# Attention loop: projections in half steps of three matmuls, other gaps between the blocks of logits

## The chip, the cores and the metric

One core of a Trainium2 chip runs the whole program. The metric is the device time of one execution in microseconds, from the median of several runs. The kernel is built with a planner (a tile framework): the program says what is computed and in which order of preference, and the planner lays out each engine's queue from its own estimate of times. Each engine then runs its queue in order, and waits at semaphores for the others. TensorE (PE) multiplies, VectorE (DVE) and ScalarE (ACT) work on results in PSUM and SBUF, SyncE (SP) issues DMAs, and GpSimd (POOL) is little used here.

## What is computed

A decoder trunk of two layers on 1024 tokens of width 1024: an RG-LRU layer, then a layer of attention with a forget gate (16 heads of 64), each with a SiLU gate, and a final RMS norm. The change is in the attention layer, of which this is the core:

```python
def one_block(args):
    q_blk, cq_blk, start = args
    qpos = start + jnp.arange(Q_BLOCK, dtype=jnp.int32)
    logits = jnp.einsum("bqhd,bkhd->bhqk", q_blk.astype(jnp.float32), kf) * scale
    logits = logits + (cq_blk[..., :, None] - ck[:, :, None, :])
    mask = kpos[None, :] <= qpos[:, None]
    logits = jnp.where(mask[None, None], logits, NEG_INF)
    p = jax.nn.softmax(logits, axis=-1)
    return jnp.einsum("bhqk,bkhd->bqhd", p, vf)

y = o * jax.nn.silu(gate)
return y @ w_out.astype(h.dtype)
```

`q`, `k`, `v` and `gate` are projections of the normed input, `ck` is a running sum of the log of the forget gate. All is float32 in the reference.

## The kernel before

Every float32 product is made of three matmuls of split operands (high times high, low times high, high times low), so that a product over 128 rows of a weight is a group of three matmuls.

**The attention loop** runs over 16 heads. For each head the 1024 queries are eight blocks of 128, and block i needs keys 0 to (i + 1) x 128. Blocks 0 to 3 are the small half, 4 to 7 the large half. The loop body of head `hd` has two calls of `run`: the first lays the large half of `hd` beside the weighting of its small half, the second lays the small half of `hd + 1` beside the weighting of the large half of `hd`. So on TensorE large and small halves alternate.

**A block of logits** is one step of the generator `maxima`: two matmuls into the PSUM tile `S` for a small block and four for a large one (by chunks of keys), mask and row maximum on VectorE (L965, output `m`), the exponential on ScalarE (`p<-S,m`), the sum's reciprocal on VectorE (L976, L977), the normalised halves `pp` (the high part on ScalarE, the low part on VectorE, L979), and a DMA transpose on SP's queue into `pT` (L982). `S` has two buffers, each of two PSUM banks, and `p` has two as well. So the logits of a block can start when the exponential two blocks earlier is through, and an exponential when the low part two blocks earlier is.

**The weighting** is the generator `weigh`: it multiplies `pT` with the values into the PSUM tile `O`, in two steps (small half) or four (large half). Its first matmul needs the transposes of all four blocks of the half.

**The fill.** Between these, TensorE makes the projections that later heads need: `play` walks over units (the gate, keys or queries of a pair of heads for 512 tokens, tile `gps`), each of 24 matmuls of 512 columns. `gemm_steps` hands control back after every second group of three, so a step is six matmuls, and a unit four steps. At the end of a unit VectorE scales its result (L692), and `use` splits it, for keys and queries into the tiles `kq` (`qkh`, `qkl`). In heads 12 to 15 the fill goes over to the last gate units, the output projection (`partial`) and `turned`.

**The order** is written out by hand, a string for each call of `run`: "1" is a block of logits, "0" a step of the weighting, "." a step of the fill. Heads 0 to 11 use `ORDER`, heads 12 to 15 `LAST`. Each step is pinned behind the last matmul issued (`tc.issue_after(pe[0].ins)`), so that TensorE's queue follows the string; the other engines' queues are the planner's.

**The loads beside it.** `side` is advanced once after each ".": it issues the loads `pieces` that copy the next heads' queries (to `U`, in the first call) and keys (to `T`, in the second) from `kq` on SP's queue, two to four DMAs a step. Each is pinned behind the transpose issued three before the latest (`turns[-lag]`, lag 3). A tile of `kq` is overwritten by a later unit only when the loads that read it are through. In heads 3, 7 and 11 `vals` (the generator `values`) is advanced behind the first and the third block of the second call: it loads and casts the weights of the next four heads' values; their 192 matmuls (`vps`) follow after that call.

**The weights.** `play` loads the next unit's weights when `i == u["load"]`, and casts them when `i` is in `u["cast"]`, where `i` counts the yields of the current unit.

Of the kernel before, what the change touches and what calls it, by code (L numbers as in the profile page):

```python
# [25 lines left out]
HD = 64  # L26
EPS = 1e-6
GROUP = 2
ORDER = "1.1..1.1..00", "1.1.1.1...0000"
LAST = "1..1..1..1..0.0", "1..1.1..1..0..0.0.0"  # L30
NEG = -1e30
PSUM = bass.MemoryType.PSUM
# [8 lines left out]
def trunk(ctx: ExitStack, tc: tile.TileContext, xt, w0, wg, wo0, pc, gn, gf, w1, wv, wf, bf, wo1, out):  # L41
# [95 lines left out]
    def gemm_steps(ps, pairs, chunks=(slice(0, HALF),)):  # L137

        pairs = list(pairs)
        for cs in chunks:  # L140
            o = ps[:, cs]
            for i, ((wh, wl), (xh, xl)) in enumerate(pairs):
                matmul(o, wh, xh[:, cs], start=i == 0, stop=False)
                matmul(o, wl, xh[:, cs], start=False, stop=False)
                matmul(o, wh, xl[:, cs], start=False, stop=i == len(pairs) - 1)
                if i % 2:
                    yield

    def drain(gen):
        for _ in gen:  # L150
# [2 lines left out]
    def take(gen, n):  # L153
        for _ in range(n):
            next(gen, None)
# [464 lines left out]
    with ExitStack() as l1:  # L620
# [49 lines left out]
        plan = []  # L670

        def job(w, h, start, use):
            u = dict(w=w, h=h, start=start, use=use, load=0, cast=(1, 2))
            plan.append(u)
            return u

# [97 lines left out]
        def kq_units(pair, parts):  # L774

            units = []
            for is_k, hs in parts:
                if hs[0] == 0 or pair == 0 or is_k and pair in (3, 5, 7):
                    kqw[is_k] = Weights(is_k * 8 + pair)

                def start(is_k=is_k, first=[True]):
                    if is_k not in kq:
                        kq[is_k] = tuple(
                            kqpool.tile([P, SEQ], F32R, tag=f"qk{p}{is_k}", name=f"qk{p}") for p in "hl"
                        )

                def use(h, pt, is_k=is_k):
                    cs = halves[h]
                    hi, lo = kq[is_k]
                    if is_k:  # L790
                        to_hi(hi[:, cs], pt, nc.scalar)
                        to_lo(lo[:, cs], pt, hi[:, cs], nc.vector)
                    else:
                        to_hi(hi[:, cs], pt, nc.scalar, scale=0.125)
                        nc.vector.scalar_tensor_tensor(lo[:, cs], pt, 0.125, f32(hi[:, cs]), ALU.mult, ALU.subtract)  # L795

                new = [job(kqw[is_k], h, start, use) for h in hs]
                for u in new:
                    u["first"], u["last"] = hs[0], hs[-1]
                    if is_k and hs == (0,) and pair in (3, 5, 7):  # L800
                        u["load"], u["cast"] = 2, (2, 3)
                units += new
            return units

# [232 lines left out]

        def run(order, *gens, fill=iter(()), side=iter(()), vals=None):

            for n, i in enumerate(order):  # L1040
                if vals and n in (1, 5):
                    with tc.issue_after(turns[-1].ins):
                        next(vals)
                if vals and n == order.rfind("1"):
                    next(vals)
                    behind[:] = loaded_last[0], cast_last[0]
                with tc.issue_after(pe[0].ins):
                    next(fill if i == "." else gens[int(i)], None)
                if i == ".":
                    next(side, None)  # L1050
            for g in gens:
                drain(g)

# [23 lines left out]
        def beside(steps, first, more):  # L1077

            for i, _ in enumerate(steps):
                if i >= first:  # L1080
                    next(more, None)
                yield

# [65 lines left out]
        def turned(c, q):  # L1149
# [14 lines left out]
            for b in range(2):  # L1164
# [4 lines left out]
                for h, (d0, nd) in enumerate(parts):  # L1169
# [6 lines left out]
                    for k in range(2):  # L1176
# [4 lines left out]
                        matmul(pt, yh, wl, start=False, stop=k == 1)  # L1181
                        if k == 0:
                            yield
                    sq = at.tile([P, HALF], F32, tag="pp", name="sq1", bufs=4)[:, : nd * P]
                    nc.scalar.activation(sq, pt, AF.Square, accum_out=ss[:, min(h, ss.shape[1] - 1)].unsqueeze(1))
                    if c == 0 or h < len(parts) - 1:
                        nc.vector.tensor_tensor(res[b][:, hs], pt, grow[d0 // 4][:, (d0 % 4) * P : (d0 % 4 + nd) * P], ALU.mult)  # L1187
                        if h == 1 and c == 1:
                            nc.vector.tensor_tensor(ss[:, 0:1], ss[:, 0:1], ss[:, 1:2], ALU.add)
                            ss = ss[:, 0::2]  # L1190
                        yield
                if c == 1:
                    r = root_mean(ss, lambda: nc.vector.tensor_tensor(res[b][:, hs], pt, grow[d0 // 4][:, (d0 % 4) * P : (d0 % 4 + nd) * P], ALU.mult))  # L1193
                    lo, hi = halves
                    nc.scalar.activation(res[b][:, lo], res[b][:, lo], AF.Copy, scale=r)
                    nc.vector.tensor_scalar(res[b][:, hi], res[b][:, hi], r, None, ALU.mult)
                    for hs in halves:
                        nc.sync.dma_start(out[4 + 2 * q + b, :, hs], res[b][:, hs])
                    yield
            if c == 0:  # L1200
                first_half.extend(res)
# [38 lines left out]
        gates1 = forget(1)  # L1240
        for _ in range(2):
            next(gates1)
            take(fill, 2)
        drain(gates1)
        drain(fill)
        fill = play(next(fills))
        for _ in range(4):
            next(fill)
        load(0, halves[1], (1,))
        load(1, halves[1], (1,))  # L1250
# [133 lines left out]
```

## Time and profile before

| | us |
|---|---|
| median of 3 runs | 1064.38 |
| lowest and highest | 1063.75, 1068.48 |
| the profiled execution's span, first to last instruction | 1057.4 |
| attention loop, heads 0 to 15, about | 506 to 1029 |
| of it heads 0 to 11, which use `ORDER`, about | 506 to 894 |

The profiled execution's whole time is its span and what lies before the first and behind the last instruction of the program. The rows of the profile that matter are shown with the prediction. How to read them: a row of the time line has the start, the duration, the engine, the line of the kernel, the operation, out<-in by the program's names, the shape, the count of instructions merged into the row, and in brackets the idle time of the engine before it and what ended that. Busy times of matmuls overlap, since they are pipelined and their ends are modelled. A row of the waits has who waited for whom, the total in us, the number of times and the longest. A row of the stretches has the stretch, its length, the busy time and count of each engine (PE, PEld, DVE, ACT, POOL), TensorE's granted clock, the share of the DMA engines and GB/s. L69 is the helper that all matmuls go through and L57 the one of all activations, so the tiles tell what an instruction is: `S<-T,U` logits, `gps<-h,w` the fill, `O<-pT,v` the weighting, `vps<-w,h` the values, `p<-S,m` an exponential, `pp<-p,sums` a normalised block.

### The profile page before, as it was taken

What the parts mean: (1) busy time and instruction counts of PE and PEld (TensorE: products, weight loads), DVE (VectorE), ACT (ScalarE), POOL (GpSimd) and SP (SyncE); (2) the same over time, 40 slices, a digit from 0 to 9 for tenths busy, and PEclk for the clock granted to TensorE, in tenths of its full rate; (3) what the DMA queues carried; (4) which work ended last, traced back from release to release, by engine and by line L of the source; (5) the groups of instructions that cost most, each with busy time, mean ns of one, the idle gap of its engine ahead of it and who ended that gap; (6) DMA issues with size and microseconds to landing.
All of it is one profiled execution on the core that took longest, in us unless ns stands there. A gap on an engine that the chain in (4) does not pass through costs nothing. (4 is left out here: it accounts for less than half of the span.)

```text
span 1057.4 us, 15071 instructions
## 1 busy us (share of the span) xinstructions
PE 1022.6 (97%) x5094; PEld 710.3 (67%) x5094; DVE 786.5 (74%) x1456; ACT 660.7 (62%) x1211; POOL 90.6 (9%) x87
## 2 busy tenths in 40 slices
PE   9999999999999999998999989999999999999997
PEld 6787878888888888765444456444754448477676
DVE  7789657667856868895879875888578875986575
ACT  8479666565657565567656755666466764854455
POOL 1311112012101120001000000000000000012100
PEclk9999999999999999999999999999999999999999
DMA  7112424233423311443688993898748985789984
GB/s 246 61 50 63 124 84 144 68 115 108 133 66 113 122 50 48 161 141 75 150 166 169 185 208 70 182 192 175 182 95 189 176 190 133 168 196 250 230 199 160
DMA packets 219806, 148.92 MB, mean 141 GB/s; under 512 B 161937, under 2 KB 174865, under 8 KB 219729
## 3 DMA queue, kind: packets, MB, share of 16 engines
q1 hardware_dynamic: 217328, 140.09, 54.0%
q0 software_dynamic: 2400, 7.87, 2.5%
q8 instruction: 40, 0.66, 0.2%
q14 instruction: 38, 0.30, 0.1%
HBM read 73.33 MB, written 11.67 MB: 80 GB/s over the span
## 5 line engine op out<-in xcount | busy, mean ns | idle before, releaser
L69 PE MATMUL gps<-h,w 128*128 128x512 f16 x1152 | 269.1, 380 | 1.3 <-DVE qkl L795 1.1
L69 PEld LDWEIGHTS <-w 128*128 128x128 f16 x1152 | 104.2, 98 | 126.8 <-issue 14.0
L57 ACT ACTIVATE p<-S,m 128x128 f32<-128x128 f32 (+7 forms) x128 | 94.4, 738 | 78.0 <-DVE m L965 32.4
L57 ACT ACTIVATE pp<-p,sums 128x128 f16<-128x128 f32 (+7 forms) x128 | 96.6, 770 | 34.9 <-DVE sums L977 22.0
L979 DVE SCALAR_TENSOR_TENSOR pp<-p,sums,pp 128x128 f16<-128x128 f32 (+7 forms) x128 | 102.5, 812 | 13.5 <-ACT pp L57 12.4
L69 PE MATMUL S<-T,U 96*128 96x512 f32 (+7 forms) x384 | 106.4, 386 | 5.2 <-ACT p L57 4.1
L965 DVE CUSTOM_DVE_ANT_0 S<-S,mask 128x128 f32<-128x128 f32 (+7 forms) x128 | 96.9, 758 | 11.8 <-PE S L69 10.5
L69 PE MATMUL vps<-w,h 128*128 128x256 f16 (+1 forms) x768 | 90.6, 280 | 11.4 <-ACT w L57 7.4
L110 POOL TENSOR_TENSOR wl<-wf,wh 128x512 fp32r<-128x512 f32 x46 | 69.3, 1511 | 324.5 <-ACT wh L57 268.5
L69 PEld LDWEIGHTS <-h 128*128 128x128 f16 x768 | 76.3, 100 | 25.9 <-issue 9.9
L69 PEld LDWEIGHTS S<-T,U 128*128 128x128 f32 (+1 forms) x384 | 66.9, 189 | 39.3 <-ACT p L57 19.1
L57 ACT CAST wh<-wf 128x512 fp32r<-128x512 f32 x88 | 51.6, 592 | 51.1 <-PE ops L69 27.6
L69 PE MATMUL ups<-hh,wh 128*128 128x512 f32 x192 | 76.2, 398 | 1.1 <-ACT hh L57 1.0
L69 PE MATMUL ops<-yh,wh 128*128 128x512 f32 x192 | 76.7, 399 | 0.6 <-ACT yh L57 0.6
L69 PE MATMUL ups<-hh,wl 128*128 128x512 f32 x192 | 75.7, 394 | 1.0 <-POOL wl L110 1.0
L69 PE MATMUL ups<-hl,wh 128*128 128x512 f32 x192 | 76.2, 397 | 0.2
L69 PE MATMUL ops<-yh,wl 128*128 128x512 f32 x192 | 75.7, 394 | 0.1
L69 PE MATMUL gps<-hh,wh 128*128 128x512 f32 x192 | 75.7, 394 | 0.1
L69 PE MATMUL gps<-hh,wl 128*128 128x512 f32 x192 | 75.5, 393 | 0.0
L69 PE MATMUL gps<-hl,wh 128*128 128x512 f32 x192 | 75.5, 393 | 0.0
L403 DVE TENSOR_TENSOR x<-x,ops 128x512 f32<-128x512 f32 x80 | 54.0, 679 | 28.2 <-PE ops L69 27.9
L69 PE MATMUL ops<-yl,wh 128*128 128x512 f32 x192 | 74.6, 394 | 0.0
(196 smaller groups left out, 1877.9 us busy)
## 6 DMA issues: line engine op xcount, KB each, us to landing
wf<-in_w SPq DMA_DIRECT2D x106, 256.0 KB
wsf<-in_w SPq DMA_DIRECT2D x48, 256.0 KB
wf<-in_wo SPq DMA_DIRECT2D x64, 128.0 KB
T<-qkh SPq DMA_DIRECT2D x64, 128.0 KB
U<-qkh SPq DMA_DIRECT2D x64, 128.0 KB
x<-in_xt SPq DMA_DIRECT2D x16, 256.0 KB
wsf<-in_wv SPq DMA_DIRECT2D x16, 256.0 KB
x1d<-x SPq DMA_DIRECT2D x16, 256.0 KB
```

The lines of the kernel that those rows point to most:

```text
L57: act[0] = op(*args, **kw)
L69: pe[0] = nc.tensor.matmul(*args, **kw)
L110: return eng.tensor_tensor(lo, src, f32(hi), ALU.subtract)
L403: nc.vector.tensor_tensor(x, x, pt, ALU.add)
L965: nc.vector.tensor_tensor_reduce(S[:, :n], S[:, :n], mask[:, SEQ - n :], -1.0, -NEG, ALU.add, ALU.min, accum_out=m)
L979: nc.vector.scalar_tensor_tensor(both[:, :, 1], p, r, both[:, :, 0], ALU.mult, ALU.subtract)
```

## The change

`gemm_steps` hands control back after every group of three matmuls, a half step. In the order strings "." stays a step (two half steps), and "," is new, one half step. `ORDER` becomes, between blocks, a step and a half, a step, a step and a half and two steps, in both calls; before it was 1, 2, 1, 2 steps in the first call and 1, 1, 1, 3 in the second. The sum is six steps in each, as before. `LAST` is unchanged. Whatever counted steps counts half steps: `load` and `cast` of the units, `beside`, the doubled yields in `turned`, the counts in front of the loop. `side` is advanced each time that the count of half steps since the start of the call is even after a "." or ",". `vals` is advanced behind the first and the third block by counting blocks.

```diff
-ORDER = "1.1..1.1..00", "1.1.1.1...0000"
+ORDER = "1.,1.1.,1..00", "1.,1.1.,1..0000"
...
                 matmul(o, wh, xl[:, cs], start=False, stop=i == len(pairs) - 1)
-                if i % 2:
-                    yield
+                yield
...
-            u = dict(w=w, h=h, start=start, use=use, load=0, cast=(1, 2))
+            u = dict(w=w, h=h, start=start, use=use, load=0, cast=(3, 5))
...
-                        u["load"], u["cast"] = 2, (2, 3)
+                        u["load"], u["cast"] = 4, (4, 6)
...
+            dots, ones = 0, 0
             for n, i in enumerate(order):
-                if vals and n in (1, 5):
+                if i == "1":
+                    ones += 1
+                if vals and (ones, i) in ((1, "1"), (3, "1")):
+                    at_ = n + 1
+                if vals and n == at_:
                     with tc.issue_after(turns[-1].ins):
                         next(vals)
                 if vals and n == order.rfind("1"):
                     next(vals)
                     behind[:] = loaded_last[0], cast_last[0]
-                with tc.issue_after(pe[0].ins):
-                    next(fill if i == "." else gens[int(i)], None)
-                if i == ".":
-                    next(side, None)
+                for _ in range(2 if i == "." else 1):
+                    with tc.issue_after(pe[0].ins):
+                        next(fill if i in ".," else gens[int(i)], None)
+                if i in ".,":
+                    dots += 2 if i == "." else 1
+                    if dots % 2 == 0:
+                        next(side, None)
...
-                if i >= first:
+                if i >= 2 * first and i % 2 == 0:
                     next(more, None)
                 yield
...
                         if k == 0:
                             yield
+                            yield
...
                         yield
+                        yield
...
                     yield
+                    yield
...
-            take(fill, 2)
+            take(fill, 4)
...
-        for _ in range(4):
+        for _ in range(8):
             next(fill)
```

## The prediction

> **What bounds the kernel now.** I read the page first, then the waits of TensorE over the attention loop (455 to 930 us), the time line of one head, and a table of stretches by head.
>
> ```profile
> span 1057.4 us, 15071 instructions
> PE 1022.6 (97%) x5094; PEld 710.3 (67%) x5094; DVE 786.5 (74%) x1456; ACT 660.7 (62%) x1211; POOL 90.6 (9%) x87
> PE vps L69 <- ACT w L57: 7.4, 3, 2.8
> PE S L69 <- ACT p L57: 4.1, 13, 0.8
> PE O L69 <- DMA pT<-pp: 3.8, 5, 1.1
> ```
>
> TensorE is busy 97% of the span, and the change takes no matmul away, so only its waits can be won. In the loop they are of three kinds: logits that wait for an exponential to free their PSUM tile (S, two buffers, so block n waits for the exponential of block n-2), the weighted values that wait for a transposed probability tile (O), and the values that wait for a cast weight (vps). The matmuls' modelled ends hide part of a wait, so I read starts instead. One small half, of head 1:
>
> ```profile
> 557.66 0.50 PE L69 MATMUL S<-T,U 128*128 128x256 f32 x2
> 558.01 1.47 PE L69 MATMUL gps<-h,w 128*128 128x512 f16 x6
> 559.13 0.59 PE L69 MATMUL S<-T,U 128*128 128x256 f32 x2
> 559.56 1.47 PE L69 MATMUL gps<-h,w 128*128 128x512 f16 x6
> 561.16 0.62 PE L69 MATMUL S<-T,U 128*128 128x384 f32 x2
> 561.62 1.47 PE L69 MATMUL gps<-h,w 128*128 128x512 f16 x6
> 563.39 0.74 PE L69 MATMUL S<-T,U 128*128 128x512 f32 x2 [0.29 <-ACT p L57]
> 563.97 4.06 PE L69 MATMUL gps<-h,w 128*128 128x512 f16 x18
> 567.87 2.44 PE L69 MATMUL O<-pT,v 128*128 128x512 f16 x16
> ```
>
> The step (six matmuls) between the first two blocks takes 558.01 to 559.13, 1.12 us. The next takes 1.60 and the third 1.77, with the same work: 0.48 and 0.65 us are waits. A block that waited then starts up a little faster, so I call the loss 1.0. Unstalled, the stretch from the first block to O is 10.21 - 1.0 = 9.2 us. The same stretch of heads 1 to 11, its first row and the sum:
>
> ```profile
> 557.66:567.87 10.21, 9.79 (x45) 4.58 (x45) 9.21 (x23) 6.64 (x15) 0.00 (x0) 1.00 0.76 152
> sum 114.40, PE 106.93 PEld 50.26 DVE 99.60 ACT 81.70 POOL 0.00; mean PE 9.72 PEld 4.57 DVE 9.05 ACT 7.43 POOL 0.00
> ```
>
> 114.40 - 11 x 9.2 = 13.2 us are lost in small halves: 1.2% of the span. VectorE is busy 9.05 of each 10.4 us there, so it isn't free either.
>
> **The change, part by part.**
>
> *The spacing in small halves.* 18 matmuls take 3.90 us, so a half step of three is 0.65. New: the third block comes 1.12 + 0.65 after the first, then 1.12 after the second: 557.66 + 0.35 + 1.77 + 0.43 + 1.12 = 561.33. The fourth comes at 561.33 + 0.47 + 1.77 = 563.57. Today they are let in at 561.16 and 563.39. If the exponentials keep their times, both waits go, by a margin of 0.17 and 0.18 only. The price is nothing: the last block's tail shrinks from three steps to two. O would start at 563.57 + 0.58 + 2.60 = 566.75 instead of 567.87.
>
> *What is late next.* The releasing chain, and O's own release:
>
> ```profile
> 550.71 1.17 PE L69 MATMUL S<-T,U 128*128 128x512 f32 x4
> 553.40 1.01 ACT L57 ACTIVATE p<-S,m 128x896 f32<-128x896 f32 x1 [1.25 <-DVE m L965]
> 557.85 1.03 ACT L57 ACTIVATE pp<-p,sums 128x896 f16<-128x896 f32 x1
> 559.61 1.15 ACT L57 ACTIVATE pp<-p,sums 128x1024 f16<-128x1024 f32 x1
> 560.66 0.35 ACT L57 ACTIVATE p<-S,m 128x128 f32<-128x128 f32 x1
> 561.45 1.28 DVE L979 SCALAR_TENSOR_TENSOR pp<-p,sums,pp 128x1024 f16<-128x1024 f32 x1
> 562.77 0.47 ACT L57 ACTIVATE p<-S,m 128x256 f32<-128x256 f32 x1 [1.05 <-DVE pp L979]
> 562.77 1.75 SPq L982 DMA_TRANSPOSE pT<-pp  x1
> 587.48 2.98 SPq L982 DMA_TRANSPOSE pT<-pp  x1
> 592.38 2.46 PE L69 MATMUL O<-pT,v 128*128 128x512 f16 x16 [0.15 <-DMA pT<-pp]
> ```
>
> The first exponential of the small half (560.66) runs behind the normalising of the large half's last block (559.61), and the second (562.77) waits until VectorE has split that block (561.45 + 1.28). The same split releases the transpose that O needs. In head 2 O waited for it and started 592.38 - 587.48 = 4.9 us after its issue. By that, head 1's is ready at 562.77 + 4.9 = 567.7 at the latest, against O's new need of 566.75: up to 0.95 of the 1.1 comes back as a wait of O. The five heads in which O waits already gain nothing from the spacing alone. So by itself this part is worth little unless the chain in front of the transpose gets shorter.
>
> *The spacing in large halves.* Half steps 2, 4, 2, 4 become 3, 2, 3, 4. The second block comes 0.65 later, the third 0.65 earlier, the fourth where it was. The third block's exponential now starts at 553.40, 2.7 us after its logits (550.71), waiting for VectorE's maxima, and its normalising waits until 557.85, in front of the last block's at 559.61. Logits 0.65 earlier should bring the transpose up to 0.65 earlier. From the other side: the second block 0.65 later in an in-order queue may push everything behind it by 0.65. ScalarE and VectorE are ordered by the planner, which may reorder around either; I take 0.65 earlier, since the last block itself does not move and ScalarE stood idle for the 1.25 us before that exponential.
>
> *The loads beside it.* `side` is now called after an even count of half steps: behind the first block, then after half steps 8, 10 and 12, so no longer behind the second block. Each call pins its loads behind the third-last transpose; being later, it pins them later. In small halves the second group of key loads moves from behind the last large transpose to behind the first small one; the others stay or move by one. No DMA is added. The place where this counts, head 3, before the values:
>
> ```profile
> 614.96 1.22 SPq L66 DMA_DIRECT2D T<-qkh  x2
> 616.23 0.59 SPq L66 DMA_DIRECT2D T<-qkl  x1
> 616.94 1.21 SPq L982 DMA_TRANSPOSE pT<-pp  x1
> 618.19 1.53 SPq L66 DMA_DIRECT2D wf<-in_wv  x3
> 621.53 0.72 ACT L57 ACTIVATE w<-wf,wsq 128x512 f16<-128x512 f32 x1 [1.74 <-DMA wf<-in_wv]
> 622.30 3.90 PE L69 MATMUL vps<-w,h 128*128 128x256 f16 x21 [2.84 <-ACT w L57]
> ```
>
> The three key loads (1.8 us of SP's queue) stand ahead of the small transpose and the value weights, whose landing sets the cast and vps. Behind them, the weights can issue up to 1.8 us sooner; nothing sooner if the transpose is bound by its own data. I take 0.8 in each of the three heads (3, 7, 11).
>
> The other end of that move: the key tile is overwritten at the head's end, and must wait for those later loads.
>
> ```profile
> 567.13 2.51 SPq L982 DMA_TRANSPOSE pT<-pp  x2
> 569.77 0.57 ACT L57 CAST qkh<-gps 128x512 fp32r<-128x512 f32 x1
> 618.84 0.69 DVE L110 TENSOR_TENSOR qkl<-gps,qkh 128x512 fp32r<-128x512 f32 x1 [0.55 <-DMA T<-qkl]
> ```
>
> Head 3 shows the wait already: the load issued at 616.23 let VectorE go at 618.84, 2.6 us later. In head 1 the loads would follow the first small transpose, at 567.13 + 1.25 = 568.4, and end their issue near 569.6; ScalarE's cast (569.77) would then be let go near 571.6, 1.8 us late, and behind it in ScalarE's queue stand the normalising of the last small blocks and the next head's first exponential. That is 0 to 1.8 us in heads 1, 5 and 9 (after 3, 7 and 11 the values hide the rest). I take 0.35 each, 1.0 together, as most of it has slack: the next block to need that exponential comes two blocks later.
>
> *The rest.* Weight casts stand after the same matmuls as before (half steps 3 and 5 for steps 1 and 2; 4 and 6 for 2 and 3 is one group of three earlier), a weight's load one half step earlier; the last four heads, `turned` and the final loop take two half steps where they took one step. Nothing: TensorE's work covers them, and POOL has no work in these stretches (0.00).
>
> **The clock.** Two of the three waits for the values are followed by a slower clock:
>
> ```profile
> 747.04 1.14 PE L69 MATMUL vps<-w,h 128*128 128x256 f16 x9 [2.39 <-ACT w L57]
> 872.22 1.03 PE L69 MATMUL vps<-w,h 128*128 128x256 f16 x8 [2.17 <-ACT w L57]
> 622.30:644.62 22.32, 22.32 (x192) 0.93 0.64 151
> 747.04:769.84 22.80, 22.71 (x192) 0.93 0.60 151
> 872.22:893.85 21.63, 21.04 (x192) 1.00 0.65 163
> ```
>
> Idle for 2.84 and 2.39 us, the 192 matmuls ran at a granted 0.93 and took 22.3 and 22.8 us; idle for 2.17, at 1.00 and 21.6. So 0.7 to 1.2 us hang on each such wait; I count none of it. The Trainium skill ("TensorE: Matmul & The Clock Gate", section "Why this matters for your kernels") asks only for no idle gaps above some 3 us; by that figure none of the three would cost clock, and the slower rival below would be 1.2 us cheaper. The trace disagrees: 2.39 us was enough.
>
> **The sum.** Of heads 1 to 11, five wait in O today (the row of waits counts five) and take what the transpose gains: 0.65 each, 3.25. Three end at the values: 0.8 each, 2.4, in place of their own 1.0. The three left lose up to 1.0 today; with O ready at 567.7 - 0.65 = 567.05 instead of 567.87, 0.8 in head 1, and 0.7 each for the three, 2.1. Head 0: 0.8, the longest S wait of the row. Minus 1.0 for the key tile. 3.25 + 2.4 + 2.1 + 0.8 - 1.0 = 7.5 us off the span of 1057.4. The execution that was profiled has its own time around that span; the median of the runs is 1064.4, 7.0 above the span, and I take that margin as unchanged: 1064.4 - 7.5 = 1056.9, rounded to 1057.
>
> **The rivals.**
> - *Full gain.* The chain shortens by more than 0.65 us, and nearly all 13.2 us of the small halves, 1 of head 0 and 2 to 3 of the values' waits go, perhaps with the clock: 1064.4 - 15 = 1049. For it: ScalarE and VectorE have idle time in large halves. Against: VectorE at 9 of 10.4 us in small ones.
> - *The wait only moves.* The transpose lands where it did; O and vps wait in place of S. Left are some 0.3 in each of the three heads that wait in neither, as much at each of the three values, and 0.8 in head 0, 2.6 in all: 1062. For it: five O waits in the row above. The case that the planner's order undoes the spacing lies here too, at no change.
> - *Slower.* The key tile's wait is not hidden: ScalarE stands 1.8 us, VectorE behind it, and the large half starts late, so that its transpose, O and the values come late with it. 1.8 in each of six odd heads, less the 2.6 of the case above, plus 1.2 of clock when the third wait passes 2.4 us: 6 x 1.8 - 2.6 + 1.2 = 9.4 slower, 1074. It turns the sign where the delay passes 0.5 us a head.
>
> **How the numbers follow.** Forecast 0.38, full gain 0.18, wait moves 0.27, slower 0.17. About 0.5%, 5.3 us, is what a measurement of this kernel tells from no change; the forecast's own range, 1053 to 1060, lies almost wholly beyond it, so faster is 0.38 x 0.95 + 0.18, rounded to 0.54; same 0.29; slower 0.17. The range leaves out the far end of each rival: 1047 to 1069.
>
> **What would show it.** Right: in small halves, steps between blocks of 1.77, 1.12 and 1.77 us with no S wait; in head 1, the third large block's exponential less than 2.7 us behind its logits; vps waits below 2.4 us and a clock of 1.00. Wrong: waits "O <- DMA pT" above 3.8 us, casts of the key tile that wait for a DMA of T, or vps waits above 2.84.

## The result and the profile after

The changed kernel takes 1066.37 us, the median of 20 runs (1063.49 to 1073.91), against 1063.99 for the kernel before in the same comparison (20 runs, 1059.96 to 1068.69). The ratio is 1.0031, 95% interval 1.0017 to 1.0044: a little slower, by about 2.4 to 3.3 us, where 7 us faster was forecast.

The two profiled executions differ by more than the kernels do. A line of the page of after, then its waits of TensorE in the attention loop, 455 to 940 us (total us, times, longest us):

```profile
PE 1022.6 (96%) x5094; PEld 712.1 (67%) x5094; DVE 782.0 (73%) x1456; ACT 661.0 (62%) x1211; POOL 96.2 (9%) x87
```

```profile
PE O L69 <- DMA pT<-pp: 12.1, 8, 3.0
PE vps L69 <- DVE v L761: 6.4, 5, 1.8
PE vps L69 <- ACT w L57: 4.5, 4, 1.9
PE S L69 <- ACT p L57: 3.8, 8, 1.6
PE S L69 <- DMA U<-qkh: 1.8, 1, 1.8
```

The spans lie 10.5 us apart (1057.4 and 1067.9), the medians 2.4: before was profiled in one of its quickest executions, after in one of its longer ones. So I compare what waits for what, not the two spans. TensorE is busy for the same 1022.6 us. The waits of S for exponentials are fewer (8 for 13), though their total hardly falls (4.1 to 3.8 us), and those of O for transposes have grown from 3.8 to 12.1 us. In the small halves of heads 1 to 11, which the spacing was made for, the time lines have ten such S waits in before, 2.8 us together, and three in after, 0.7 us; the longest S wait of after, 1.6 us, lies in a large half. Head 1's small half, in the time line of after (start, duration, engine, line, instruction, idle time before it):

```profile
558.09 0.51 PE L69 MATMUL S<-T,U 128*128 128x256 f32 x2
558.44 2.12 PE L69 MATMUL gps<-h,w 128*128 128x512 f16 x9
560.20 0.59 PE L69 MATMUL S<-T,U 128*128 128x256 f32 x2
560.63 1.47 PE L69 MATMUL gps<-h,w 128*128 128x512 f16 x6
561.75 0.70 PE L69 MATMUL S<-T,U 128*128 128x384 f32 x2
562.29 2.12 PE L69 MATMUL gps<-h,w 128*128 128x512 f16 x9
564.05 0.81 PE L69 MATMUL S<-T,U 128*128 128x512 f32 x2
568.90 1.40 PE L69 MATMUL O<-pT,v 128*128 128x512 f16 x6 [1.44 <-DMA pT<-pp]
```

The steps between the blocks last 1.76, 1.12 and 1.76 us (558.44 to 560.20, 560.63 to 561.75, 562.29 to 564.05) and no block waits. Then O waits 1.44 us. From the first block to O it is 10.81 us, where before it was 10.21. Over heads 1 to 11 the stretch sums up so (columns as in the prediction):

```profile
sum 119.09, PE 105.95 PEld 52.11 DVE 107.23 ACT 85.51 POOL 0.00; mean PE 9.63 PEld 4.74 DVE 9.75 ACT 7.77 POOL 0.00
```

119.09 us against 114.40 before: the stretch that was to shrink has grown. Without O's own waits it shrinks, from 110.6 to 107.0. What held O in head 1: first two rows of before that the prediction doesn't show, then the time lines of TensorE, ScalarE, VectorE and SP's queue in after:

```profile
545.49 0.95 PE L69 MATMUL S<-T,U 128*128 128x320 f32 x4
556.13 1.11 ACT L57 ACTIVATE p<-S,m 128x1024 f32<-128x1024 f32 x1 [0.65 <-DVE sums L976]
```

```profile
545.95 0.93 PE L69 MATMUL S<-T,U 128*128 128x320 f32 x4
550.50 1.18 PE L69 MATMUL S<-T,U 128*128 128x512 f32 x4
552.97 1.01 ACT L57 ACTIVATE p<-S,m 128x896 f32<-128x896 f32 x1 [1.34 <-DVE sums L976]
556.00 1.04 ACT L57 ACTIVATE pp<-p,sums 128x896 f16<-128x896 f32 x1 [0.62 <-ACT sg L57]
556.95 1.10 ACT L57 ACTIVATE p<-S,m 128x1024 f32<-128x1024 f32 x1
559.48 0.37 ACT L57 ACTIVATE p<-S,m 128x128 f32<-128x128 f32 x1
559.84 1.14 ACT L57 ACTIVATE pp<-p,sums 128x1024 f16<-128x1024 f32 x1
561.68 1.28 DVE L978 SCALAR_TENSOR_TENSOR pp<-p,sums,pp 128x1024 f16<-128x1024 f32 x1
560.94 0.91 SPq L66 DMA_DIRECT2D U<-qkh  x1
563.02 0.48 SPq L66 DMA_DIRECT2D T<-qkh  x1
563.61 3.87 SPq L981 DMA_TRANSPOSE pT<-pp  x2
```

The large half of head 1 began at 545.95 here and at 545.49 before; I count from there. The third block (896 columns) gained: its logits start at +4.55, before at +5.22; its exponential at +7.02, before at +7.91; its normalising at +10.05, before at +12.36. The last block (1024 columns), on which O hangs, did not: its exponential starts at +11.00 instead of +10.64, since the third block's normalising now stands ahead of it. The small half's first exponential (559.48) has slipped in ahead of the last block's normalising (559.84). VectorE's split ends at +17.01 instead of +17.24, 0.23 us earlier. SP issues the transpose at +17.66 instead of +17.28, later by 0.38: when the split was done (562.96) SP was at the end of a row of loads for U and T, and one more load of T (563.02) went out ahead of the transpose. In before the T loads of that moment stood behind it (564.57). O starts 5.29 us behind that issue.

### The profile page after: what moved, and what is told of

Read it like the earlier page. It is cut to its first block, busy times and chain, and to the rows that moved or that the text cites. A ratio compares the mean times of both kernels' runs of the same rounds, so it can differ in the third digit from the quotient of the medians.

```text
span 1067.9 us, 15058 instructions
## 1 busy us (share of the span) xinstructions
PE 1022.6 (96%) x5094; PEld 712.1 (67%) x5094; DVE 782.0 (73%) x1456; ACT 661.0 (62%) x1211; POOL 96.2 (9%) x87
## 5 line engine op out<-in xcount | busy, mean ns | idle before, releaser
L110 POOL TENSOR_TENSOR wl<-wf,wh 128x512 fp32r<-128x512 f32 x46 | 74.8, 1630 | 319.9 <-ACT wh L57 263.5
L646 DVE SCALAR_TENSOR_TENSOR w<-wf,wsq,w 128x512 f16<-128x512 f32 (+1 forms) x74 | 54.7, 746 | 30.4 <-ACT w L57 29.4
```

Source lines behind the costliest of these rows:

```text
L110: return eng.tensor_tensor(lo, src, f32(hi), ALU.subtract)
L646: nc.vector.scalar_tensor_tensor(lo, wt, scales[:, b : b + 1], hi, ALU.mult, ALU.subtract)
```

## The experiments

What waits had moved was plain; what held the transposes was not. Three causes were tried apart: ScalarE's and VectorE's order (the chain in front of the transpose), the later loads and casts of `side`, and the transfers themselves, that is SP's one queue and the DMA engines behind it (the last is theory D). The letters in the expectations name theories; the first expectation with a letter says what it means. All kernels were timed in five rounds beside the kernel before; each ratio is to that. "Old strings" is `ORDER` of before written for the new `run`: `"1.1..1.1..00", "1.1.1.1...0000"`.

### Each string by itself (e1, e2, e3)

```diff
-ORDER = "1.,1.1.,1..00", "1.,1.1.,1..0000"
+ORDER = "1.1..1.1..00", "1.1.1.1...0000"       # e1: both old
+ORDER = "1.1..1.1..00", "1.,1.1.,1..0000"      # e2: new in small halves only
+ORDER = "1.,1.1.,1..00", "1.1.1.1...0000"      # e3: new in large halves only
```

> The changed kernel with the old order strings: half steps and the new counting, the gaps of before. Three theories of the 2.4 us (1063.99 to 1066.37). A, the wait moves: logits that come later free TensorE of the S waits, but the transpose of the last large block lands no sooner, so O waits instead. B, the loads: `side` is advanced later, the loads and weight casts come late on SP's queue. C, the backlog: two steps instead of three behind the last small block push its work into the next large half. All three expect this one at the kernel before, 1064 within 1.5 us, with S waits of 22 us (PEld row) and O waits near 4 us as before. If it is slower by 2 us or more, it is the half steps themselves (one pin a group instead of one a step, a weight load one group earlier), and not the gaps.

> Only the small halves have the new gaps (step and a half, step, step and a half, two); the large halves keep 1, 2, 1, 2. A: S waits gone (PEld row from 18.5 to under 9 us), O waits up from 3.8 to 8 us or more, time 1062 to 1065. B: near 1065 to 1066, because `side` is late in this call, which holds the key loads. C: 1065 to 1067, the first maxima of even heads come 1 us later after their logits than before.

> Only the large halves have the new gaps (step and a half, step, step and a half, two); small halves keep 1, 1, 1, 3. A: S waits stay (18 us in the PEld row), O waits fall to 2 us or less if earlier logits of the third block bring the transpose sooner, time 1061 to 1064. B: 1064 to 1066, the query loads are late but the key loads are not. C: 1063 to 1065, the tail of three steps is kept, so no backlog.

Measured: e1 1063.63 us, ratio 1.0004 (0.9985 to 1.0024); e2 1066.57, 1.0026 (1.0010 to 1.0041); e3 1066.44, 1.0032 (1.0014 to 1.0051). The machinery of half steps costs nothing; the spacing does. Either string alone costs about as much as both together. O's waits, 500 to 905 us, in e1, e2 and e3:

```profile
PE O L69 <- DMA pT<-pp: 4.9, 5, 1.3
PE O L69 <- DMA pT<-pp: 7.2, 6, 2.4
PE O L69 <- DMA pT<-pp: 3.5, 5, 1.3
```

e1 has the order of before and was profiled in its longest execution (span 1068.1), so 4.9 in place of 3.8 is about what the spread of executions does to this row; the 12.1 of after is beyond it, and so are the 9.4 to 10.6 of e4, e14 and e18. In e2 the S waits all but go (1.0 us in two, against 4.0 in thirteen in e1), and O's grow: the wait moves. e3 is the nearest test of the spacing in large halves. O's five waits fall by 1.4 us together, and the S waits grow to 8.6 us in nineteen. No theory had e3 as slow as this (1061 to 1066).

### The side work at its old pace (e4)

With new strings the even counts of half steps fall later. e4 calls `side` as soon as two more half steps have run.

```diff
-                    if dots % 2 == 0:
+                    if dots // 2 > stepped:
+                        stepped += 1
                         next(side, None)
```

> The changed kernel with its gaps, but `side` advanced once for every whole step done (each time that the half steps pass an even count), as often and about as early as before. B: back to 1064 or below, ScalarE's casts wait for weights 9 us instead of 15.5 and O waits fall by 4 us or more. A and C: 1065.5 to 1067, O waits still above 9 us.

Measured: 1065.83 us, 1.0023 (0.9999 to 1.0048). Its longest waits, 500 to 905 us, are those of O: nine, 9.4 us together. ScalarE's waits for the weights of the projections are hardly shorter, 13.3 us against 13.7 in after over the same stretch. The pace of `side` alone is worth half a microsecond, within the uncertainty.

### O put off (e5, e6)

If O's wait is all that is wrong, weigh the values later. In nine heads the weighting of the large half runs inside the next head's first half (e5, with the pace of e4); e6 does the same with the old string in small halves and the pace of after. The edit is shortened here: the new generator `weighed_late` and what `maxima` needs to put its first transpose behind that weighting are left out.

```diff
             if was_late:
+                first = '1.22221.,1.,1..00'
             if is_late:
+                second = second.replace("0", "")
-            run(first, weigh(hd, 0), maxima(hd, 1), fill=fill, side=side)
+            run(first, weigh(hd, 0), maxima(hd, 1, was_late), *([weighed_late(hd - 1)] if was_late else []), fill=fill, side=side)
-            run(second, weigh(hd, 1), maxima(hd + 1, 0), fill=fill, side=side, vals=vals)
+            run(second, iter(()) if is_late else weigh(hd, 1), maxima(hd + 1, 0), fill=fill, side=side, vals=vals)
```

> The gaps of the change in small halves, `side` advanced once a step, and the weighting of the large half put off past the next head's first large block and one step (2.0 us more for its transpose), in the heads that no values follow (0, 1, 2, 4, 5, 6, 8, 9, 10). Theory A (the freed S waits only moved to O, whose transpose lands 1 to 2.3 us behind the need): with O out of the way both kinds of wait go, O waits in these heads under 1 us in all, 1054 to 1058. Rival C (the loop goes at the pace of VectorE's and ScalarE's queues, and TensorE waits for them wherever its order puts the wait): O waits go, but the logits of the next large half wait in their place, 1061 to 1066.

> The same delay of the weighting, with the small halves' old gaps (1, 1, 1, 3) and the large halves as in e5_late_O_new. A: S waits stay (some 0.5 to 1 us a head), O waits go (4.6 us in all), 1057 to 1060, and 2 to 4 us slower than e5_late_O_new. C: 1061 to 1066 like the other, the two within 1.5 us of each other.

Measured: e5 1062.44 us, 0.9988 (0.9971 to 1.0005); e6 1064.03, 1.0018 (0.9997 to 1.0038). The waits of TensorE in e5, 500 to 905 us:

```profile
PE vps L69 <- ACT w L57: 10.2, 3, 3.7
...
PE O L69 <- DMA pT<-pp: 4.4, 4, 1.9
```

O waits for 4.4 us in place of 12.1, and the values wait for their weights for 10.2 in place of 4.5. e5 is 0.35% below e4, which has the same pace of `side`, and so back at the time of before, not below it as theory A had it (1054 to 1058). I read it so: room at O let TensorE come sooner to the next transfer that is late.

### A third of the loads left out (e7, e8)

Each head copies twelve pieces of 128 KB into T and U by SP's queue. e7 (new strings) and e8 (old) leave out four of them, the second copy of the keys' and queries' high part, so that the low-order products read an older head's rows.

```diff
             for i, (to, from_) in enumerate((todo[3], *todo[:3])):
-                piece(f32(to), from_, lag)
+                if i != 2:
+                    piece(f32(to), from_, lag)
```

> The changed kernel without the second copy of the high part of keys and queries in `pieces` (one of three 128 KB loads left out, four a head, some 0.5 MB; the logits then read an older head's values in those rows, so the output isn't the reference's). Theory D: the pace is set by SP's queue and the DMA engines, which are 0.9 busy in these heads, so that TensorE's waits come back wherever a transpose or a weight lands last. D: O waits fall from 12.1 to under 4 us, time 1050 to 1058, and 3 us or more below e8_two_loads_old, since the S waits are gone there. C (VectorE and ScalarE set the pace): 1063 to 1067, O waits above 8 us.

> The same loads left out, with the old order strings. D: the O waits (3.8 us) and some of the values' go, S waits stay near 18 us in the PEld row, 1056 to 1061. C: 1061 to 1064.

Measured beside the same executions of before: e7 1046.15 us, 0.9848 (0.9822 to 0.9875); e8 1053.65, 0.9936 (0.9913 to 0.9959). Waits of e7, then of e8, 500 to 905 us:

```profile
PE vps L69 <- ACT w L57: 3.7, 4, 1.5
PE O L69 <- DMA pT<-pp: 2.5, 5, 0.6
PE S L69 <- ACT p L57: 1.0, 2, 0.8
```

```profile
PE vps L69 <- ACT w L57: 6.6, 3, 2.3
PE S L69 <- ACT p L57: 3.9, 13, 0.8
```

With a third of the copies gone the sign turns: the new spacing is 7.5 us faster than the old. The S waits go from 13 to 2, and O's waits are short. Both times are below what theory D gave (1050 to 1058 and 1056 to 1061). So with fewer copies about the spacing pays. Not all of the 7.5 us is its own doing: the stretch from the first small block to O, summed over heads 1 to 11, is 106.81 us in e7 and 109.48 in e8, 2.67 less. Another 2.9 us lie in the waits for the values' weights, and one stretch at half clock follows such a wait in e8 (622 to 626 us), none in e7.

### The values' weights one transpose earlier (e9, e10, e14)

In heads 3, 7 and 11 the loads of the values' weights are pinned behind the latest transpose; these kernels pin them behind the one before it. e9 has old strings, e14 new ones, e10 is e5 with this edit.

```diff
-                    with tc.issue_after(turns[-1].ins):
+                    with tc.issue_after(turns[-2].ins):
                         next(vals)
```

> The old order strings, with the loads of the value weights pinned one transpose earlier (behind the large half's last instead of the small half's first), so ahead of the key loads on SP's queue. Theory V: the three waits for the values, and the slower clock behind them, collect what the heads in front win, because the loads' place is fixed. V: the wait for the value weights falls from 7.4 to under 3 us, no clock below 1.00 behind them, 1056 to 1060. If the wait stays above 6 us or the time within 1.5 us of 1063.5, the weights are not held by their place in the queue.

> e5_late_O_new (new gaps in small halves, weighting put off) with the value weights' loads pinned one transpose earlier. V: what e5_late_O_new won in the heads comes out at last, 1050 to 1056, and at least 3 us below e9_values_early_old. D: 1057 to 1062, the wait moves on to O or to the logits of the heads before the values.

> The changed kernel with the value weights' loads pinned one transpose earlier, as in e9_values_early_old (1054.5). If the new gaps are worth nothing while the loads are as many (D), 1055 to 1060, no faster than e9_values_early_old, O waits above 8 us. If the values alone collected the gain (V), 1048 to 1053.

Measured: e9 1054.45 us, 0.9929 (0.9901 to 0.9958); e10 1066.08, 1.0033 (1.0014 to 1.0052); e14 1065.98, 1.0014 (0.9990 to 1.0038). Against the before beside it e9 wins 8.0 us, without any room made in the queue; the values wait for their weights for 0.5 us there. With the new strings the same edit does nothing. e10 and e14 lie above every range that was given for them (1050 to 1062 and 1048 to 1060). In e10 the values wait for VectorE's copies instead, 9.9 us in three waits.

### Four of the twelve copies on another engine or queue (e11, e12)

Both have the new strings and leave nothing out. e11 makes four of the twelve copies of a head with GpSimd, SBUF to SBUF; e12 keeps four as DMAs but issues them from GpSimd's queue.

```diff
-                piece(f32(to), from_, lag)
+                if is_k and i == 2:                              # e11
+                    nc.gpsimd.tensor_copy(to, f32(t[:64, 0, cs]))
+                elif not is_k and i == 1 + s:
+                    nc.gpsimd.tensor_copy(to, from_)
+                else:
+                    piece(f32(to), from_, lag)
```

```diff
-                piece(f32(to), from_, lag)
+                if i == 2:                                       # e12
+                    nc.gpsimd.dma_start(f32(to), from_)
+                else:
+                    piece(f32(to), from_, lag)
```

> The changed kernel, all of it computed, with four of the twelve 128 KB loads a head made by copies on GpSimd, which stands idle: the second high part of the keys (from the tile's own first part) and the one high part of the queries that stays on its partitions. Theory D: as many DMAs less as in e7_two_loads_new, so the same freedom for transposes and weights, 1046 to 1052, O waits under 4 us. Rival: GpSimd's copies come late or slow VectorE (its busy time up by 3% or more, the maxima longer than before), 1056 to 1066.

> The changed kernel with the second high parts still loaded by DMA, but issued from GpSimd's queue in place of SP's: SP issues as few as in e7_two_loads_new, the DMA engines move as much as before. If SP's queue is what holds transposes and weights (D1), 1046 to 1054. If the DMA engines are (D2), 1062 to 1068, O waits above 8 us.

Measured beside the same executions of before: e11 1050.28 us, 0.9874 (0.9847 to 0.9901); e12 1057.54, 0.9939 (0.9917 to 0.9960). Off SP's queue but with the same bytes, about half of the gain comes (7.2 of 14.5 us against their 1064.77); off the DMA engines too, the rest. In the stretch 656 to 745 us (busy time of PE, PEld, DVE, ACT, POOL, then clock, DMA share, GB/s), after and then e12:

```profile
656.00:745.00 89.00, 83.38 (x409) 42.07 (x408) 72.39 (x180) 58.09 (x109) 0.00 (x0) 0.98 0.85 172
```

```profile
656.00:745.00 89.00, 84.78 (x435) 44.30 (x436) 75.04 (x187) 60.43 (x116) 7.20 (x14) 1.00 0.93 192
```

e12 drives the DMA engines harder (0.93 against 0.85) and is faster than after: what holds the transposes is not the engines' share alone, but also their place in SP's order. That is argued from one stretch. One caveat: the four loads of e12 and the four copies of e11 are no longer pinned behind a transpose, so they also move; e7 keeps its pins.

### The spacing once more, with nothing left out (e13, e15, e16, e17)

Now the copies of e11 with the other edits: e17 old strings; e13 new strings and e15 old strings, both with the values' weights early; e16 is e13 with the pace of e4. The edits are those shown above.

> e11_copies_on_pool_new with the value weights' loads pinned one transpose earlier. D and V add up: 3 to 8 us below e11_copies_on_pool_new, 1040 to 1048. If the copies already freed the queue for the value weights: within 2 us of e11_copies_on_pool_new.

> The strings of before, with 4 of the 12 loads of a head turned into GpSimd copies, as in e11 (which ran at 1050.28 against 1064.77, ratio 0.987, with the new strings). Nothing is left out of the computation, so the pair e11 and e17 says what the new gaps are worth when fewer transfers stand between the transposes. Theory D (the transfers on SP's queue and the DMA engines hold the last transposes, and while they do, the waits that the gaps take away come back as others): the gain of the gaps seen between e8 and e7 (7.5 us, 0.7%) is here too, so 1054 to 1060, ratio 0.991 to 0.997. Theory P (the pair e7/e8 gained by chance of which loads fell away, or because the copies free VectorE or ACT in other ways; the gaps are worth nothing): as e11 within 2 us, 1048 to 1052, ratio 0.986 to 0.989.

> As e17, with the values' weight loads issued one transpose earlier (the edit of e9, which alone gave 9 us with the old strings and nothing with the new ones: e14, and e13 beside e11). With old strings the third small block's wait for its exponentials stays, so PE falls behind a little before the values' part and the late weights hurt; theory D expects the two remedies to overlap: 1050 to 1056, below e17 by 0 to 5 us. If they add in full (9 us on top of e17's 1054 to 1060) it would come to 1045 to 1051, below e13's 1050.99, and the gaps would then be a loss beside the values' loads, not a gain.

> e13 (new strings, copies on GpSimd, values' loads one transpose earlier: 1050.99) with the weights' side work at the first chance after two half steps rather than at the end of the second string's pairs (the edit of e4, which alone moved after by -0.5 us). Theory D, in which the queue's load is gone and only PE's small waits are left, expects -1 to 0 us: 1050 to 1051, ratio 0.987 to 0.988. A theory by which the weights' casts, late in after, are what is left would have 3 us: the vps and gps waits for w in e11 are 3.9 us over eight heads, so 1047 to 1048.

Measured: e13 1050.99 us, 0.9880 (0.9856 to 0.9905). Beside other executions of before, e17 1058.26, 0.9963 (0.9949 to 0.9977); e15 1048.93, 0.9876 (0.9860 to 0.9893); e16 1044.06, 0.9825 (0.9807 to 0.9843). The expectation of e16, -1 to 0 us against e13, was a miss: the pace of `side`, worth nothing in e4, is worth 0.55% here. VectorE's waits of e13, 500 to 905 us, show a likely reason:

```profile
DVE qkl L110 <- DMA T<-qkl: 12.0, 6, 2.7
```

Six times VectorE stood, up to 2.7 us, for a load of T that was still to read the key tile. In e16 that is 1.4 us in three waits.

e15 and e16 have the same loads, copies and weights; the old strings call `side` after every two half steps, as e16 does, so only the spacing differs. The stretch from the first small block to O, summed over heads 1 to 11, in e15 and in e16:

```profile
sum 111.47, PE 106.47 PEld 50.51 DVE 97.24 ACT 79.47 POOL 7.24; mean PE 9.68 PEld 4.59 DVE 8.84 ACT 7.22 POOL 0.66
```

```profile
sum 105.80, PE 102.96 PEld 51.52 DVE 98.58 ACT 77.52 POOL 12.71; mean PE 9.36 PEld 4.68 DVE 8.96 ACT 7.05 POOL 1.16
```

5.67 us less, and the medians differ by 4.9. The granted clock is the same in both (a mean of 0.998 over the executions), so this is the cleanest pair for the spacing. With the pace of after it is worth nothing here: e13 has a ratio of 0.9880 and e15 of 0.9876, and e15 lies below its range of 1050 to 1056. The pair e11 and e17 is less clean: they differ by 0.9% in the ratio, but the same sum is 111.55 in e11 and 111.45 in e17, so that difference does not lie in the small halves. In e17 the values wait 7.8 us for weights, in e11 3.9, and TensorE falls to half clock in three places in the loop of e17 (from 622, 746 and 990 us on), in none in that of e11. Over the executions the mean granted clock is 0.995 in e17 and 0.998 in e11. The expectation there took the right size for the wrong place.

### Is it the weights or the transfers? (e18)

e18 is e16 with all twelve copies back on SP's queue.

> e16 without the copies on GpSimd: the new strings, the values' loads one transpose earlier and the side work after every two half steps, with all twelve loads of a head back on SP. e16 ran at 0.9825 of before; taking either edit alone to after gave nothing (e4 1.0023, e14 1.0014). Theory D (the number of transfers on SP and the DMA engines holds the last transposes, whatever the weights do): O waits on pT near the 9 to 11 us of e4 and e14 again, ratio 0.998 to 1.003, 1060 to 1065 us. Theory W (the lateness of the weights, values' loads and side casts together, is the cause, and the copies were only another way to make room for it): most of e16's gain, ratio 0.983 to 0.990, 1044 to 1051 us. Between them, 0.990 to 0.998, both are needed in part.

Measured: 1065.98 us, 1.0015 (0.9994 to 1.0036). Theory D holds, W falls: with the new strings and without the room in the queue the two edits do nothing. Head 3, where the values follow the small half, shows how a gain is given back. SP's queue and TensorE in e9 (old strings, same early weights), in e18, and in e16:

```profile
614.22 2.87 SPq L981 DMA_TRANSPOSE pT<-pp  x1
617.14 1.52 SPq L66 DMA_DIRECT2D wf<-in_wv  x3
619.33 2.44 PE L69 MATMUL O<-pT,v 128*128 128x512 f16 x16
621.70 13.55 PE L69 MATMUL vps<-w,h 128*128 128x256 f16 x120
```

```profile
612.64 4.68 SPq L981 DMA_TRANSPOSE pT<-pp  x2
617.38 1.52 SPq L66 DMA_DIRECT2D wf<-in_wv  x3
617.62 2.44 PE L69 MATMUL O<-pT,v 128*128 128x512 f16 x16 [0.69 <-DMA pT<-pp]
621.72 10.77 PE L69 MATMUL vps<-w,h 128*128 128x256 f16 x96 [1.66 <-ACT w L57]
```

```profile
611.57 3.65 SPq L986 DMA_TRANSPOSE pT<-pp  x2
615.27 1.52 SPq L66 DMA_DIRECT2D wf<-in_wv  x3
616.01 2.44 PE L69 MATMUL O<-pT,v 128*128 128x512 f16 x16
619.58 10.77 PE L69 MATMUL vps<-w,h 128*128 128x256 f16 x96 [1.12 <-ACT w L57]
```

With the new spacing TensorE reaches O at 617.62 instead of 619.33, 1.7 us sooner. But the two transposes hold SP for 4.68 us, the weights go out at 617.38, not sooner than in e9 (617.14), and the values start at 621.72 against 621.70. The equal start is in part chance, since 0.7 of the 1.7 us was there at the loop's first logits (507.32 against 508.04), before the new order could act. Nor does e18's loss against e9 lie here: its values start 5.4 us later in head 7 and 13.3 later in head 11 (749.12 and 878.23 against 743.69 and 864.89), and in heads 4 to 11 O waits for 8.1 us, against 2.6 in e9. In e16, with fewer transfers about, the transposes hold SP for 3.65 us, and weights and values come 2.1 us earlier.

All ratios together, by string and by what stands beside it:

| beside the strings | old strings | new strings, pace of after | new strings, pace of e4 |
|---|---|---|---|
| nothing | 1.0004 (e1) | 1.0031 (after) | 1.0023 (e4) |
| values' weights early | 0.9929 (e9) | 1.0014 (e14) | 1.0015 (e18) |
| copies on GpSimd | 0.9963 (e17) | 0.9874 (e11) | not run |
| both | 0.9876 (e15) | 0.9880 (e13) | 0.9825 (e16) |

e16 beats both kernels, by 1.75% against before.

## Why the prediction was wrong

*The S waits of small halves go.* Right in the main, by rows: blocks 1.76, 1.12 and 1.76 us apart where 1.77, 1.12 and 1.77 were worked out, and no S wait in head 1 in spite of margins of 0.17 and 0.18 us. The stretch itself was taken a little short: in head 3 of after, where nothing waits inside it, it is 9.33 us, not 9.2.

*What is late next.* Right in kind, O's wait for the last large transpose, but too small: "up to 0.95 of the 1.1 comes back" became 1.44 us in head 1, and 12.1 us in eight waits for 3.8 in five.

*The spacing in large halves.* **This is the step that failed**: "Logits 0.65 earlier should bring the transpose up to 0.65 earlier." In head 1 the third block's logits did come 0.67 us earlier and its exponential 0.89. But the transpose that O needs is the last block's, and that was not behind the third block in one fixed line. The planner filled the time won with other work ahead of the last block, so that its split ended only 0.23 us earlier. And the transpose goes out when SP's queue comes to it, which was 0.38 us later. The prediction followed ScalarE and VectorE and let SP follow at once; it listed SP's queue for the values, not for the transposes. Where the string of the large halves is changed alone (e3 against e1), O's five waits fall by 1.4 us in place of the 3.25 forecast for five heads.

Nor does room in the queue bring the whole of it. In e16 the last transpose of head 1 goes out at +17.09, 0.19 us earlier than in before:

```profile
562.49 4.23 SPq L986 DMA_TRANSPOSE pT<-pp  x2
```

O starts 5.48 us behind it, at 567.97, and waits 1.05 us; the prediction had taken 4.9 from issue to O. On this step hung 3.25 us in the five heads where O waits (2, 4, 6, 8 and 10) and 2.1 in heads 1, 5 and 9, 5.35 together. By the stretches of e16 against e15 the five heads win 2.14 us and the three 0.93, so 3.07. The other 2.60 of the 5.67 lie in heads 3, 7 and 11, for which the prediction counted only the loads. That 5.67 is close to 5.35 is chance.

*Head 0.* The 0.8 us was the longest S wait of before, 0.85 at 531.73. It doesn't go: 0.83 at 533.08 in after, and 0.83 in e16 as well.

*The loads beside it.* The forecast was 2.4 us from the values. The wait of the values for weights did fall, 7.4 to 4.5 us, and that for VectorE's copies rose, 3.9 to 6.4: together 11.3 to 10.9, so 0.4. The sign set for this part came true (no wait for weights above 1.9 us, and a clock of 1.00 behind them), and so did that for the third large block (2.47 us from logits to exponential, where less than 2.7 was asked). Neither sign asked whether the time won arrives at the next transfer. The prediction looked only at the loads that stood ahead of the values' weights; it left out that everything `side` issues later lands later. ScalarE's waits for the weights of the projections went from 8.9 us in five (455 to 930 us) to 15.5 in nine (to 940 us). One of these, at the end of head 1, delays the next head's first maxima from 0.98 to 2.11 us behind the start of its logits, and O of that head then waits 1.89 us. No run mends this alone: e4 was meant to, but its waits for these weights are as long (13.3 us).

*The key tile.* 1.0 us was charged, and in after it is not to be seen: VectorE's wait for T's loads is 0.5 us there, 2.1 before. The mechanism exists: in e13 it is 12.0 us in six waits.

*The clock.* Left out of the sum, and it doesn't explain the result. In the profiled executions two stretches of some 3.4 us at half clock fall into the loop of before and three into that of after, in other places. Over the executions the mean granted clock is 0.995 in after (20) and 0.994 in before (130, those timed beside the experiments). It goes with about half of the spread: over these 130 a clock lower by 0.001 comes with 1.0 us more. Estimated by that figure, some 3.5 of the 9 us between e11 and e17 is clock, and 2 of the 3 us between e1 and e2 (means of 0.9940 and 0.9921), so that the equal losses of e2, e3 and after need not have one cause.

*The span and the runs.* "7.0 above the span" was taken as a margin around the execution. Much of it was the spread of the executions: that of after took 1069.69 us around a span of 1067.9, 1.8 more, and by the same margin that of before took some 1059.2, below the lowest of its 20 runs (1059.96). The step cancels in the difference, but it hid that the trace came from a quick execution; in that of e1, with the same order, O waits 4.9 us in place of 3.8 and the values 8.9 for their weights in place of 7.4.

*The rivals.* "The wait only moves" came nearest: O and the weights wait in place of S. It had 2.6 us left over as a gain; the result is a loss of about that size, which it didn't foresee. The "slower" rival named the key tile; in after the one such delay that I followed, at the end of head 1, comes by way of late weights. What stays open is why after is 0.2 to 0.3% slower rather than equal, and why either string alone costs about as much as both. The rows show waits for transposes, U and weights that exceed the S waits won. e5 takes most of O's wait away, and the loss against before with it, but brings other waits; no run makes the waits for U or for the weights go by themselves.

## What to carry to other kernels

When a wait is spaced away, follow the next one through every queue to the transfer that releases it: the gain is real only if that transfer can go out earlier, and here a queue that carries transposes and copies in one order could not send it earlier. Try such a change a second time after the shared resource has been relieved; here the same spacing is worth between +0.9% (e18 against e9) and -0.5% (e16 against e15). And an edit that does nothing by itself can pay behind another: the pace of `side` is worth nothing in e4 and 0.55% in e16 against e13.

## What the runs showed of the hardware

*A transpose's time on its queue isn't fixed.* Two in a row hold SP's queue for 4.68 us in e18 and for 3.65 in e16, at the same place in head 3; the row of e9 has one of 2.87.

*Copies on GpSimd cost the other engines little.* The copies of e11 (64 x 512) in 500 to 905 us, with count, total, mean ns and the idle time before them:

```profile
L837 POOL CAST T<-T 64x512 fp32r<-64x512 f32 x25 | 19.5, 781 | 294.7 <-DMA T<-qkh 264.2 <-PE gps L69 30.6
L839 POOL CAST U<-qkh 64x512 fp32r<-64x512 f32 x24 | 16.1, 669 | 88.8 <-PE S L69 72.8 <-ACT qkh L57 9.6 <-issue 6.1
```

0.7 to 0.8 us each, on an engine that had no work in these stretches, and the page of e11 has VectorE busy for 786.4 us and ScalarE for 659.7, against 782.0 and 661.0 in after, which has the same strings.

*The length of an idle stretch alone doesn't decide the clock.* The prediction read that 2.39 us were enough and 2.17 not. In after, O started behind a wait of 2.98 us in head 6 and of 2.03 in head 4; the 3.4 us that follow (columns as above, the clock stands before the last two):

```profile
723.23:726.70 3.47, 3.47 (x22) 1.87 (x23) 0.94 (x2) 1.41 (x2) 0.00 (x0) 1.00 0.60 129
669.72:673.13 3.41, 3.41 (x12) 1.31 (x13) 1.16 (x2) 0.72 (x1) 0.00 (x0) 0.54 0.69 137
```

No slow clock after 2.98 us, and 0.54 after 2.03. A third such stretch of after, at 998 to 1001 us, has 0.50 behind a wait of 1.82 us. The Trainium skill ("TensorE: Matmul & The Clock Gate", section "Why this matters for your kernels") asks for no idle gaps above some 3 us; the second row disagrees. The same page, section "What's actually happening", has the activity watched in free-running windows of about 3.4 us; by that the place of a gap counts beside its length, which fits the two rows and their 3.4 us, but no run here shifts a gap to test it.
